# Turning the left halves of three normalized residuals by DMA instead of on TensorE

## The chip, the cores and the metric

The kernel runs on one core of a Trainium2 chip. The metric is device time in microseconds. Five engines work side by side, each through its own queue of instructions in order, and meet by semaphores: TensorE (PE in the profile, with its weight loads as PEld), VectorE (DVE), ScalarE (ACT), GpSimd (POOL) and SyncE (SP), whose queue here issues nearly all DMAs.

## What is computed

One decoder layer on 256 tokens of width 2048, in float32. The residual h passes a half SwiGLU, a mixing block (a gated MLP and sliding-window attention side by side), a cross-attention to 256 memory rows, a second half SwiGLU and a final norm:

```python
def reference(x, mem, ...):
    h = x
    for l in range(DEPTH):                                   # DEPTH = 1
        h = h + 0.5 * swiglu(rmsnorm(h, g_ffn1[l]), w1_gate[l], w1_up[l], w1_down[l])
        z = rmsnorm(h, g_mix[l]) @ w_in[l]
        ...
        h = h + y @ w_out[l]
        h = h + cross_attention(rmsnorm(h, g_x[l]), rmsnorm(mem, g_mem[l]),
                                w_xq[l], w_xkv[l], w_xo[l])
        h = h + 0.5 * swiglu(rmsnorm(h, g_ffn2[l]), w2_gate[l], w2_up[l], w2_down[l])
    return rmsnorm(h, g_final)
```

Three of these norms matter here. The kernel calls their results n2 (g_mix, between the down projection f1d of the first SwiGLU and the projection q), n3 (g_x, between the output projection wo of the mixing block and the query projection xq) and n4 (g_ffn2, between xo, the output projection of the cross-attention, and f2g, the gate and up projection of the second SwiGLU).

## The kernel before

**Matrix products.** A product with a weight is cut into *units* of 1024 output columns, and a unit into *chunks*: one chunk is 256 rows of the weight as four blocks of 128x512, 1 MB, loaded by SP. Full precision is had by splitting each operand into a high and a low part: ACT casts a weight block to wh (L147), DVE subtracts to get wl (L148), and three matmuls are done (high by high, low by high, high by low). Of the weights three chunks can be loaded ahead, and two can be cast ahead. The other operand is a *pair*: two 128-row pieces of the transposed activations, four 128x128 blocks, again as high and low parts (names with fh and fl, for n2 n2fh and n2fl).

**Kinds of chunks.** N is the plain product of two-by-two blocks (24 matmuls). S is a chunk by seven products in the manner of Strassen (21 matmuls); it needs sums of weight blocks (DVE makes t from L337 to L341, ACT casts it to th, DVE makes tl) and sums of activation blocks. C stands between them. In an S chunk, and in the first and last chunk of a unit, the third matmul already reads wl; in the others the wl passes come last. wo has two units of eight chunks, with the kinds NNNNNSNN and NNNSNSNN; xo has the same. The last unit of f1d has the kinds NNSNSNN.

**PSUM.** Eight banks: four for results that are read at a unit's end, four ("tr") for the products that are read early and for transposes. At the end of a unit DVE adds the results to h. The products P1, Q5, Q6 and Q7 of S chunks are read early: ACT copies P1 (wop, L627), DVE forms wov and woz from it and adds them to h (names f1dp, f1dv, f1dz in f1d; xop, xov, xoz in xo).

**The norms.** next_norm builds n2, n3 and n4 as the columns of h become final. A unit of f1d, wo or xo finishes one half of h: the first (columns 0 to 1023, blocks j = 0 and 1) is ready one unit before the other. When the left half is final, its squares give a provisional scale; scaled(j) multiplies 512 columns of h by it on ACT (L834, tile n2s, n3s or n4s), and make(j) turns them: for each of two pairs PE makes four transposes of 128x128 (L248, against ident), and ACT brings them from PSUM with the gain (L266). So while the last unit of f1d, wo or xo runs, four pairs of the left half are made beside it; the four of the right half follow in the next unit.

**Order.** PE's order is that of the code (it alone is pinned). Two lists set where other work goes in it. Side work (side_add) is run in steps between groups of six matmuls. The list later holds pairs of a count and a function; turn, called once a chunk, runs those whose count is 0 and takes 1 from the others. On ACT, DVE, POOL and SP a scheduler sets the order of instructions when the program is built; on the chip each queue keeps it.

**Turning by DMA, as f1 does it already.** The results of gate and up, and the memory keys, are not transposed on PE: turned_rows splits each float32 into two 16-bit halves on ACT (L153, a 128x1024 copy), SP issues a transposing DMA (L156), and two 128x512 copies a pair (L691) put the halves together again.

Of the kernel before, what the change touches and what calls it, by code (L numbers as in the profile page):

```python
# [33 lines left out]
def layer_kernel(  # L34
# [43 lines left out]
    def s2(s):  # L78
        return tmp.tile([P, 512], F32, tag="s2", name=nm(s))
# [84 lines left out]
    def words_of(raw, n):  # L164
        return raw.bitcast(U16).rearrange("p (i t h) -> p i t h", i=n, h=2)
# [74 lines left out]
    def laid(kind, k, tb):  # L240
        return BASE[kind].index(f"A{tb + 1}{k + 1}")
# [9 lines left out]
    def row_tile(kind, v, k):  # L251

        return v[:, k::2, :] if kind == "C" else v[:, 2 * k:2 * k + 2, :]

    def pair_from_rows(s, kind, src, gcol):
        ps = transposed(s, kind, src)
        p = Pair(s, kind)
        if kind != "N":
            raw = s2(s + "r").rearrange("p (k t) -> p k t", k=4)
        for k in range(2):  # L260
            g = sm[:, gcol + k:gcol + k + 1]
            if kind == "N":
                hi, lo = [row_tile("N", t, k) for t in p.base]
                split_scaled(hi, lo, row_tile("N", ps, k), g)
            else:
                nc.scalar.activation(row_tile(kind, raw, k), row_tile(kind, ps, k), AF.Copy, scale=g)  # L266
        if kind != "N":
            fill(s, p, raw)
        return p
# [171 lines left out]
    def side_add(gen):  # L441
        side.append([now[0], gen])
# [357 lines left out]
    def next_norm(s, gcol, kinds="NNNNNNNN"):  # L800

        mixed = "S" in kinds
        parts = tiny.tile([P, TB, NG], F32, tag="parts", name=nm("parts"))
        pairs = [None] * 8
        done = [0] * NG
        st = {}  # L810

        def on_block(j, tb):
            square_into(parts[:, tb, j:j + 1], h[:, tb, j * 512:(j + 1) * 512], 512)
            done[j] += 1
            if not mixed:
                if done[j] == TB:
                    make(j, lambda tb, c: h[:, tb, c:c + P])
            elif j < 2:
                if done[0] + done[1] == 2 * TB:
                    st["est"] = rstd_of(parts[:, :, :2], 2, 1024)  # L820

                    def first():
                        yield 1
                        for i in range(2):
                            scaled(i)

                    side_add(first())
            elif done[j] == TB:
                scaled(j)

        def scaled(j):
            r = m4(s + "s").rearrange("p (b c) -> p b c", b=TB)
            for tb in range(TB):
                nc.scalar.activation(  # L834
                    r[:, tb], h[:, tb, j * 512:(j + 1) * 512], AF.Copy, scale=st["est"][:, tb:tb + 1]
                )
            make(j, lambda tb, c: r[:, tb, c - j * 512:c - j * 512 + P])

        def make(j, src):
            def work():  # L840
                for i in (2 * j, 2 * j + 1):
                    yield 4 if i % 2 == 0 and mixed else 1
                    pairs[i] = pair_from_rows(
                        s, kinds[i], lambda tb, k: src(tb, (2 * i + k) * P), gcol + 2 * i
                    )

            side_add(work())

        def rs():
            if "rs" not in st:  # L850
                st["rs"] = rstd_left(parts, st["est"]) if mixed else rstd_of(parts, NG, D)
            return st["rs"]

        return pairs, on_block, rs
# [655 lines left out]
```

## Time and profile before

| | |
|---|---|
| median of 3 runs | 2034.7 us (2034.1 to 2034.9) |
| the profiled execution | 2033.6 us, span 2031.9 us |
| granted TensorE clock | 0.999 |
| instructions on PE, DVE, ACT | 9203, 1994, 1460 |
| DMA | 415.83 MB, mean 205 GB/s |

The span runs from the first to the last instruction of the profiled execution; its own time is 1.7 us longer. Three stretches of it matter: the end of f1d (about 655 to 715 us from the start), the end of wo (1088 to 1150) and the end of xo (1290 to 1372). Rows of a timeline give start, duration, engine, line, operation, output and inputs; the bracket at the end tells how long the engine was idle before, and what ended that. Instructions on one engine overlap a little, so what one costs in its queue is read from the next one's start.

### The profile page before, as it was taken

The page shows a single profiled execution, that of the slowest core. Times are in us where ns is not written, and L with a number is a line of the kernel's source. Part 1 is how long each engine was busy: PE and PEld are TensorE (multiplying, and loading weights), DVE is VectorE, ACT ScalarE, POOL GpSimd, SP SyncE. Part 2 cuts the span into 40 slices and gives each one's busy share as a digit, 9 for nine tenths or more (in the row PEclk, how much of TensorE's full clock was granted, in tenths as well). Part 3 has the DMA queues.
Part 4 walks back from the last instruction along what each step waited for, and adds up shares of the span by engine and source line. Part 5 has one row for each costly group of instructions (what it writes and reads, how often), then busy time and mean ns, then how long its engine had stood idle before and what let it go on. Part 6 is the DMA issues. An engine that isn't in the chain of part 4 may idle for free.

```text
span 2031.9 us, 24271 instructions
## 1 busy us (share of the span) xinstructions
PE 2015.5 (99%) x9203; PEld 1668.8 (82%) x9203; DVE 1853.6 (91%) x1994; ACT 1313.2 (65%) x1460; POOL 34.4 (2%) x57
## 2 busy tenths in 40 slices
PE   9999999999999999999999999999999999999998
PEld 7788888888888888888888888888888888888886
DVE  6999999999999978989879987899999999999998
ACT  7765566567665766755566666676656666676664
POOL 0000000000000010200000000000000000000000
PEclk9999999999999999999999999999999999999999
DMA  8666666666556575544675544556566656665563
GB/s 312 197 206 225 215 218 205 236 209 220 196 191 219 177 252 178 202 166 166 208 227 182 198 160 145 187 187 224 197 239 215 215 205 231 214 219 206 187 228 125
DMA packets 115333, 415.83 MB, mean 205 GB/s; under 512 B 61824, under 2 KB 63888, under 8 KB 68112
## 3 DMA queue, kind: packets, MB, share of 16 engines
q1 hardware_dynamic: 112768, 407.14, 57.6%
q0 software_dynamic: 2016, 6.30, 1.0%
q8 instruction: 72, 1.18, 0.2%
q10 hardware_dynamic: 432, 0.84, 0.1%
q14 instruction: 45, 0.37, 0.1%
HBM read 398.52 MB, written 2.10 MB: 197 GB/s over the span
## 4 chain that ended last, share of the span: by engine, by line
PE 85%; DVE 9%; issue 3%; ACT 2%; DMA 2%; SPq 0%; POOL 0%; POOLq 0%; DVEq 0%; ACTq 0%
PE f1gQ L428 12%; PE f2gQ L428 12%; PE f2dQ L428 6%; PE f1dQ L428 6%; PE f1gP L428 5%; PE f2gP L428 4%; PE xqQ L428 3%; PE f2dP L428 3%; PE f1dP L428 3%; PE woQ L428 2%; PE xoQ L428 2%; PE f2dR L428 2%; PE f1dR L428 2%; DVE f1gwl L148 2%; PE vQ L428 2%
## 5 line engine op out<-in xcount | busy, mean ns | idle before, releaser
L148 DVE TENSOR_TENSOR f1gwl<-f1gw,f1gwh 128x1536 fp32r<-128x1536 f32 (+2 forms) x94 | 181.6, 1934 | 24.5 <-ACT f1gwh L147 23.8
L147 ACT CAST f2gwh<-f2gw 128x1536 fp32r<-128x1536 f32 (+1 forms) x88 | 150.5, 1712 | 66.4 <-PE f2gQ L428 44.9
L148 DVE TENSOR_TENSOR f2gwl<-f2gw,f2gwh 128x1536 fp32r<-128x1536 f32 (+1 forms) x88 | 179.1, 2036 | 8.0 <-ACT f2gwh L147 8.0
L147 ACT CAST f1gwh<-f1gw 128x1536 fp32r<-128x1536 f32 (+2 forms) x94 | 153.1, 1629 | 45.0 <-PE f1gQ L428 19.3
L147 ACT CAST f1gth<-f1gt 128x1024 fp32r<-128x1024 f32 x76 | 79.9, 1051 | 103.1 <-DVE f1gt L337 68.7
L147 ACT CAST f2gth<-f2gt 128x1024 fp32r<-128x1024 f32 x82 | 85.4, 1050 | 64.2 <-DVE f2gt L341 34.0
L428 PE MATMUL f2gQ<-f2gwh,n4fh 128*128 128x512 f32 x317 | 123.8, 390 | 0.6 <-DVE f2gv L587 0.6
L428 PE MATMUL f2gQ<-f2gwh,n4fl 128*128 128x512 f32 x317 | 123.4, 389 | 0.0
L428 PE MATMUL f1gQ<-f1gwh,n1fl 128*128 128x512 f32 x286 | 111.4, 390 | 1.7 <-DVE n1fl L148 1.7
L428 PE MATMUL f1gQ<-f1gwh,n1fh 128*128 128x512 f32 x286 | 111.6, 390 | 0.0
L147 ACT CAST f2dwh<-f2dw 128x2048 fp32r<-128x2048 f32 (+1 forms) x44 | 77.4, 1758 | 47.5 <-PE f2dQ L428 39.5
L147 ACT CAST f1dwh<-f1dw 128x2048 fp32r<-128x2048 f32 (+1 forms) x44 | 77.3, 1757 | 43.7 <-PE f1dQ L428 42.7
L148 DVE TENSOR_TENSOR f1dwl<-f1dw,f1dwh 128x2048 fp32r<-128x2048 f32 (+1 forms) x44 | 92.0, 2092 | 12.0 <-ACT f1dwh L147 11.8
L148 DVE TENSOR_TENSOR f2dwl<-f2dw,f2dwh 128x2048 fp32r<-128x2048 f32 (+1 forms) x44 | 92.0, 2091 | 11.2 <-ACT f2dwh L147 11.1
L148 DVE TENSOR_TENSOR f2gtl<-f2gt,f2gth 128x1024 fp32r<-128x1024 f32 x82 | 99.5, 1218 | 1.0
L428 PE MATMUL f2gQ<-f2gwl,n4fh 128*128 128x512 f32 x317 | 96.7, 389 | 0.0
L148 DVE TENSOR_TENSOR f1gtl<-f1gt,f1gth 128x1024 fp32r<-128x1024 f32 x76 | 92.2, 1216 | 0.5
L428 PE MATMUL f1gQ<-f1gwl,n1fh 128*128 128x512 f32 x286 | 86.9, 389 | 0.0
L428 PEld LDWEIGHTS f2gQ<-f2gwh,n4fh 128*128 128x128 f32 x317 | 59.5, 188 | 13.8 <-DVE f2gv L587 1.6
L428 PEld LDWEIGHTS f2gQ<-f2gwh,n4fl 128*128 128x128 f32 x317 | 59.5, 188 | 12.2
L428 PEld LDWEIGHTS f2gQ<-f2gwl,n4fh 128*128 128x128 f32 x317 | 59.4, 188 | 12.3
L428 PE MATMUL f2gP<-f2gwh,n4fh 128*128 128x512 f32 x176 | 68.6, 390 | 0.0
(824 smaller groups left out, 6072.2 us busy)
## 6 DMA issues: line engine op xcount, KB each, us to landing
f2gw<-in_w_gu SPq DMA_DIRECT2D x88, 1024.0 KB, 4.9
f1gw<-in_w_gu SPq DMA_DIRECT2D x86, 1024.0 KB, 4.8
f1dw<-in_w_down SPq DMA_DIRECT2D x44, 1024.0 KB, 4.8
f2dw<-in_w_down SPq DMA_DIRECT2D x44, 1024.0 KB, 4.8
wow<-in_w_out SPq DMA_DIRECT2D x16, 1024.0 KB, 4.8
xqw<-in_w_xq SPq DMA_DIRECT2D x16, 1024.0 KB, 4.8
xow<-in_w_xo SPq DMA_DIRECT2D x16, 1024.0 KB, 4.8
qw<-in_w_in SPq DMA_DIRECT2D x8, 1024.0 KB, 4.8
```

The source lines that it names most:

```text
L147: nc.scalar.copy(hi, src)
L148: nc.vector.tensor_tensor(lo, src, hi.bitcast(F32), ALU.subtract)
L428: nc.tensor.matmul(self.banks[name], x, y, start=name not in self.begun, stop=self.left[name] == 0)
```

## The change

The left halves of n2, n3 and n4 take the way by DMA. scaled(j) for j = 0 and 1 calls turned_rows for both token blocks instead of make; a new function pair_joined puts the halves together, scales them by the gain in place, and fills the pair. These steps are no side work any more: scaled(0) and scaled(1) are put in the list later with the counts 0 and 1, and each puts its two pairs there with the counts 1 and 2. The right halves are made as before. Lines behind the new function move by 21 or 27 (L627 becomes L648, L834 becomes L850).

```diff
+    def pair_joined(s, kind, turned, c, gcol):
+        raw = s2(s + "r")
+        words = words_of(raw, 4)
+        for tb in range(TB):
+            j, k = laid(kind, 0, tb), laid(kind, 1, tb)
+            nc.scalar.copy(words[:, j:k + 1:k - j], by_block(turned)[:, tb, c:c + 2])
+        raw = raw.rearrange("p (k t) -> p k t", k=4)
+        p = Pair(s, kind)
+        for k in range(2):
+            g = sm[:, gcol + k:gcol + k + 1]
+            src = row_tile(kind, raw, k)
+            if kind == "N":
...
+            else:
+                nc.scalar.activation(src, src, AF.Copy, scale=g)
+        if kind != "N":
+            fill(s, p, raw)
+        return p
...
                     st["est"] = rstd_of(parts[:, :, :2], 2, 1024)
-                    def first():
-                        yield 1
-                        for i in range(2):
-                            scaled(i)
-                    side_add(first())
+                    for i in range(2):
+                        later.append((i, lambda i=i: scaled(i)))
...
-            make(j, lambda tb, c: r[:, tb, c - j * 512:c - j * 512 + P])
+            if j > 1:
+                make(j, lambda tb, c: r[:, tb, c - j * 512:c - j * 512 + P])
+                return
+            t = tile_turned(s + "t")
+            for tb in range(TB):
+                turned_rows(s, t[:, tb], r[:, tb])
+            def pair(i):
+                pairs[i] = pair_joined(s, kinds[i], t, 2 * (i % 2), gcol + 2 * i)
+            for i in (2 * j, 2 * j + 1):
+                later.append((1 + i % 2, lambda i=i: pair(i)))
```

**What moves on the engines.** On PE 48 transposes go, 16 in each of the three places, and the rest keeps its order. On ACT and DVE the scheduler's order changes around them. First ACT in the last unit of f1d, when the left half of h is final: n2s is the scaled left half, f1dwh_5286 (before) and f1dwh_5315 (after) the cast of the weights of chunk 2, an S chunk. Before:

```order
L147 CAST f1dwh_5246<-f1dw_5245 128x2048
L834 ACTIVATE n2s_5267<-h,rs_5243 128x512 x2
L834 ACTIVATE n2s_5270<-h,rs_5243 128x512 x2
L147 CAST f1dwh_5286<-f1dw_5285 128x1536
L147 CAST f1dth_5299<-f1dt_5289 128x1024
L147 CAST f1dwh_5362<-f1dw_5361 128x2048
```

The same place after the change; n2w are the 16-bit halves, n2t what the transposing DMA writes, n2r the halves joined:

```order
L147 CAST f1dwh_5256<-f1dw_5255 128x2048
L850 ACTIVATE n2s_5245<-h,rs_5243 128x512 x2
L153 COPY n2w_5249<-n2s_5245 128x1024
L153 COPY n2w_5252<-n2s_5245 128x1024
L850 ACTIVATE n2s_5289<-h,rs_5243 128x512 x2
L153 COPY n2w_5293<-n2s_5289 128x1024
L153 COPY n2w_5296<-n2s_5289 128x1024
L277 COPY n2r_5299<-n2t_5248 128x512
L147 CAST f1dwh_5315<-f1dw_5314 128x1536
L147 CAST f1dth_5328<-f1dt_5318 128x1024
```

Four copies and one that waits for a transposing DMA now stand between n2s and the S chunk's cast.

Second, DVE at the end of wo, before: wov and woz come from the early products, the last four adds to h (from woP, woQ, woR and woQ) are the results of the unit's last chunk, and xqwl is the low part of the first weights of the next unit, xq.

```order
L628 SCALAR_TENSOR_TENSOR wov_9118<-woQ_1806_9026,wop_1818_9117 128x512
L621 SCALAR_TENSOR_TENSOR h<-woQ_1804_9024,h 128x512
L631 SCALAR_TENSOR_TENSOR woz_9119<-woQ_1805_9025,wov_9118 128x512
L621 SCALAR_TENSOR_TENSOR h<-woQ_1804_9024,h 128x512
L639 TENSOR_TENSOR h<-h,wov_9118 128x512
L640 TENSOR_TENSOR h<-h,woz_9119 128x512
L641 TENSOR_TENSOR h<-h,woz_9119 128x512
L148 TENSOR_TENSOR xqwl_9161<-xqw_9159,xqwh_9160 128x2048
L621 SCALAR_TENSOR_TENSOR h<-woP_1757_8839,h 128x512
L621 SCALAR_TENSOR_TENSOR h<-woQ_1758_8840,h 128x512
L621 SCALAR_TENSOR_TENSOR h<-woR_8841,h 128x512
L621 SCALAR_TENSOR_TENSOR h<-woQ_1760_8842,h 128x512
```

DVE at the same place after the change, from woz on:

```order
L652 SCALAR_TENSOR_TENSOR woz_9123<-woQ_1809_9029,wov_9122 128x512
L232 TENSOR_TENSOR n3f_9013<-n3r_9004,n3f_9013 128x128
L659 TENSOR_TENSOR h<-h,wop_1822_9121 128x512
L660 TENSOR_TENSOR h<-h,wov_9122 128x512
L642 SCALAR_TENSOR_TENSOR h<-woP_1763_8851,h 128x512
L642 SCALAR_TENSOR_TENSOR h<-woQ_1764_8852,h 128x512
L148 TENSOR_TENSOR n3fl_9010<-n3f_9013,n3fh_9009 128x512
L661 TENSOR_TENSOR h<-h,woz_9123 128x512
L662 TENSOR_TENSOR h<-h,woz_9123 128x512
L642 SCALAR_TENSOR_TENSOR h<-woR_8853,h 128x512
L642 SCALAR_TENSOR_TENSOR h<-woQ_1766_8854,h 128x512
L148 TENSOR_TENSOR xqwl_9165<-xqw_9163,xqwh_9164 128x2048
```

xqwl has moved from ahead of the last four adds to behind them, and pieces of the last left pair (n3f, n3fl) stand among them. At the end of xo the order changes in the same way, with f2gwl in xqwl's place; at the end of f1d qwl keeps its place ahead of the adds.

Third, ACT at the end of wo before, where wowh are the casts of chunks 6 and 7 and xqwh is the first cast of xq:

```order
L147 CAST wowh_9091<-wow_9090 128x2048
L627 ACTIVATE wop_1818_9117<-woP_1803_9023 128x512
L147 CAST wowh_9130<-wow_9129 128x2048
L147 CAST xqwh_9160<-xqw_9159 128x2048
L137 ACTIVATE junk_9190,parts_8415<-h 128x512
```

The same place after:

```order
L147 CAST wowh_9095<-wow_9094 128x2048
L147 CAST n3fh_8950<-n3r_8947 128x512
L147 CAST n3fh_8952<-n3f_8956 128x256
L277 COPY n3r_9004<-n3t_8882 128x2x256 x2
L147 CAST wowh_9134<-wow_9133 128x2048
L287 ACTIVATE n3r_9004<-n3r_9004,sm 128x256 x2
L147 CAST xqwh_9164<-xqw_9163 128x2048
L147 CAST n3fh_9007<-n3r_9004 128x512
L648 ACTIVATE wop_1822_9121<-woP_1807_9027 128x512
```

The evacuation wop, which DVE's wov waits for, has moved from behind chunk 6's cast to behind xqwh. On SP the four transposing DMAs of each norm go among the weight loads: one, a load, then three in a row.

More of the change, by code (lines that the diff above doesn't have):

```diff
@@ L266, in pair_from_rows @@
                 nc.scalar.activation(row_tile(kind, raw, k), row_tile(kind, ps, k), AF.Copy, scale=g)
+        if kind != "N":
[13 more added lines that the diff above has]
+            if kind == "N":
+                hi, lo = [row_tile("N", t, k) for t in p.base]
+                split_scaled(hi, lo, src, g)
+            else:
+                nc.scalar.activation(src, src, AF.Copy, scale=g)
         if kind != "N":
```

## The prediction

> **What bounds the kernel now.** The page first: busy time by engine.
>
> ```profile
> span 2031.9 us, 24271 instructions
> PE 2015.5 (99%) x9203; PEld 1668.8 (82%) x9203; DVE 1853.6 (91%) x1994; ACT 1313.2 (65%) x1460; POOL 34.4 (2%) x57
> ```
>
> PE is idle for 16 us of the span, so a microsecond less of matmul is a microsecond less of time, as long as nothing makes PE wait. DVE at 91% and ACT at 65% feed it: each chunk of weights is cast by ACT (wh), and DVE makes the remainder (wl). Next, PE's timeline where left halves are transposed now, at the end of f1d's last unit (start, duration, instruction):
>
> ```profile
> 672.52 0.62 PE L428 MATMUL f1dP<-f1dwl,f1afh 128*128 128x512 f32 x2
> 672.98 0.60 PE L248 MATMUL n<-ident,n2s 128*128 128x128 f32 x4
> 673.34 0.70 PE L428 MATMUL f1dQ<-f1dwl,f1afh 128*128 128x512 f32 x2
> 673.88 0.63 PE L428 MATMUL f1dR<-f1dwl,f1afh 128*128 128x512 f32 x2
> ...
> 675.16 0.48 PE L428 MATMUL f1dP<-f1dwh,f1afh 128*128 128x512 f32 x1
> 675.48 0.40 PE L428 MATMUL f1dP<-f1dwh,f1afl 128*128 128x512 f32 x1
> 675.71 0.40 PE L428 MATMUL f1dP<-f1dwl,f1afh 128*128 128x512 f32 x1
> ```
>
> Starts tell more than durations: a pair of 512-wide matmuls costs 672.98 - 672.52 = 0.46 us, one 0.23. A group of four transposes holds the queue for 673.34 - 672.98 = 0.36, and the pair behind it takes 673.88 - 673.34 = 0.54, 0.09 too long: **0.45 us a group**. At 675.16 an S chunk begins, and its third matmul, 0.55 later, already reads wl. So a late wl stops PE at once.
>
> **What the change takes away.** Twelve groups (four pairs in each of n2, n3, n4): 12 x 0.45 = 5.4 us of PE. The view of the transposes' tile adds who waits for them:
>
> ```profile
> L248 PE MATMUL n<-ident,n4s x32: 270/272/276, 1302.8 to 1351.4; 128*128 128x128 f32 x32
>   PEld xoQ L428: 1.6, 1
> ```
>
> Of these 32 half go. The one wait is in xo's S chunk, which needs a PSUM bank that n4's evacuation holds; the next rows show it, and a wait in q for its second chunk's cast.
>
> ```profile
> 1314.16 0.39 PE L428 MATMUL xoQ<-xoth,xofl 128*128 128x512 f32 x1
> 1315.72 0.50 PE L428 MATMUL xoQ<-xoth,xofh 128*128 128x512 f32 x1 [1.17 <-ACT n4r L266]
> ...
> 707.30 0.39 PE L428 MATMUL qQ<-qwl,n2fh 128*128 128x512 f32 x1
> 707.88 0.50 PE L428 MATMUL qP<-qwh,n2fh 128*128 128x512 f32 x1 [0.19 <-ACT qwh L147]
> ```
>
> 1.56 - 0.23 = 1.3 us goes with the bank; 0.58 - 0.23 = 0.35 goes if PE reaches that chunk later, as it will below. **Taken away: 7.1 us.**
>
> A rule stands against the change: the Trainium skill, VectorE: DVE Perf Modes, section Rules for kernel authors, says to transpose 128x128 on TensorE where PSUM will do. With the 390 ns of its section The three transpose paths, 48 would be worth an estimated 18.7 us, and the sum below would come out 4 us faster. The rows above give 0.11 us each; the trace decides, and the sum keeps 5.4.
>
> **What it adds.** Per norm, ACT gets four copies of 128x1024 halves and eight of 128x512; the scalings only change their source. SP gets four transposing DMAs. Prices from their like in f1 and mk:
>
> ```profile
> 226.78 1.04 ACT L153 COPY f1w<-f1gp 128x1024 uint16<-128x1024 uint16 x1
> 227.72 1.04 ACT L153 COPY f1w<-f1gz 128x1024 uint16<-128x1024 uint16 x1
> 482.07 1.85 ACT L691 COPY f1r<-f1a 128x512 uint16<-128x512 uint16 x3
> f1a<-f1w SPq DMA_TRANSPOSE x22, 3.2
> L156 SPq DMA_TRANSPOSE mkT<-mkw x8: 1237/1316/4127, 1005.5 to 1054.2; - x8
> DMA to landing us min/median/max: 3.2/5.3/6.6
> ```
>
> A large copy takes 0.94 us of ACT's queue (start to start), a small one 0.6: 4 x 0.94 + 8 x 0.6 = 8.6 us a norm. ACT has such idle time on average, but not where the copies stand. I follow the queue at each place.
>
> *n2, the S chunk.* Rows of ACT, then DVE:
>
> ```profile
> 667.65 2.57 ACT L834 ACTIVATE n2s<-h,rs 128x512 f32<-128x512 f32 x4 [0.55 <-POOL rs L132]
> 670.12 1.46 ACT L147 CAST f1dwh<-f1dw 128x1536 fp32r<-128x1536 f32 x1
> 671.62 1.76 DVE L148 TENSOR_TENSOR f1dwl<-f1dw,f1dwh 128x1536 fp32r<-128x1536 f32 x1 [2.19 <-ACT f1dwh L147]
> ```
>
> Now the cast begins at 670.12; in the changed order four copies and one L277 copy stand ahead of it: 667.65 + 2.47 + 4 x 0.94 + 0.6 = 674.5. It ends at 676.0, wl at 676.0 + 1.76 = 677.75. PE, rid of two groups, wants wl at 675.71 - 0.90 = 674.8. **Stall 2.95 us.** Behind the cast wait the T casts and chunk 3's wh (679.3, wanted at 682): no more stalls there. The L277 copy needs the first transposing DMA, issued about 670.1, landed at 673.3 by the 3.2 above and 676.7 by the longest 6.6; I take the short one, as only one load overlaps, and keep 2.8 us for the range. SP's loads pass: each issue is 1.3 us of its queue (4.1 at most), the next loads are wanted 10 us later.
>
> *n2, the unit's end.* What a piece costs on ACT and where q begins on PE:
>
> ```profile
> 674.54 0.82 ACT L266 ACTIVATE n2r<-n,sm 128x256 f32<-128x256 f32 x2
> 675.40 0.62 ACT L147 CAST n2fh<-n2r 128x512 fp32r<-128x512 f32 x1
> 679.01 1.05 ACT L147 CAST f1dth<-f1dt 128x1024 fp32r<-128x1024 f32 x1
> 702.09 0.39 PE L428 MATMUL qP<-qwh,n2fh 128*128 128x512 f32 x1
> ```
>
> f1dp (the evacuation of product P1) had its place right behind chunk 5's cast; now all pair work and q's first cast stand ahead of it. From 679.3 on that is four pairs of n2r (0.8 each), three more weight casts (1.4, 1.8, 1.8), two f1dth (0.95), seven n2fh (0.5 or 0.3), six L277 copies (0.6): 16.7 us, to 696.0; then q's cast 1.8 and f1dp 0.6: 698.5. DVE, which has qwl to do first (to 700.4), needs f1dv, f1dz, a remainder and two adds before it reads f1dP's bank, free at 704.05. PE wants that bank for q at 702.09 - 1.8 + 2.95 = 703.2, so it waits 0.85, and 0.25 more for the last bank. **1.1 us**, the upper end; the lower is 0, with the bank free in time.
>
> *n3, wo to xq.* Same steps: the S chunk first.
>
> ```profile
> 1098.11 2.56 ACT L834 ACTIVATE n3s<-h,rs 128x512 f32<-128x512 f32 x4
> 1109.51 0.39 PE L428 MATMUL woP<-wowl,yafh 128*128 128x512 f32 x1
> ```
>
> 1098.11 + 6.85 = 1104.95, cast to 1106.4, wl to 1108.3; wanted at 1109.51 - 1.8 = 1107.7. Stall 0.6. Then the end of wo, DVE's and PE's rows:
>
> ```profile
> 1129.86 2.28 DVE L148 TENSOR_TENSOR xqwl<-xqw,xqwh 128x2048 fp32r<-128x2048 f32 x1
> 1132.06 0.68 DVE L621 SCALAR_TENSOR_TENSOR h<-woP,h 128x512 f32<-128x512 f32 x1
> 1132.66 0.68 DVE L621 SCALAR_TENSOR_TENSOR h<-woQ,h 128x512 f32<-128x512 f32 x1
> ...
> 1135.10 0.69 DVE L621 SCALAR_TENSOR_TENSOR h<-woQ,h 128x512 f32<-128x512 f32 x1 [0.67 <-PE woQ L428]
> 1134.90 0.39 PE L428 MATMUL xqP<-xqwh,n3fh 128*128 128x512 f32 x1
> 1135.35 0.39 PE L428 MATMUL xqP<-xqwl,n3fh 128*128 128x512 f32 x1
> 1127.85 1.92 ACT L147 CAST xqwh<-xqw 128x2048 fp32r<-128x2048 f32 x1 [4.61 <-PE woQ L428]
> ```
>
> Before, xqwl is done ahead of the last four adds to h. In the changed order **it stands behind them**, and the last add can't start before wo's last matmul. So even a punctual DVE makes PE wait: add at 1135.10, xqwl at 1135.7 to 1138.0, against 1135.35: 2.7 us, the lower end. DVE isn't punctual: wop stands behind xqwh on ACT, which PE releases at 1127.85 - 1.1 = 1126.7 and which ends at 1128.5; a cast of n3fh and wop follow, to 1129.6. Then on DVE, 0.6 each for wov, woz and two adds, 0.2 for two small n3f (1132.5), seven more of 0.6 (1136.75), xqwl 2.28: 1139.0. PE has ended wo at 1133.8 and wants wl at 1134.25. Stall 4.8, the value I take, as every row of its walk is from this place. **n3: 5.5** with 0.1 for the chunk before.
>
> *n4, xo to f2g.* The same orders, 202.4 us later, and f2gwl behind the adds too. ACT and DVE have more to do here:
>
> ```profile
> 1300.50 2.56 ACT L834 ACTIVATE n4s<-h,rs 128x512 f32<-128x512 f32 x4
> ...
> 1308.84 0.40 ACT L147 CAST n4more<-n4d 128x256 fp32r<-128x256 f32 x1
> 1327.07 1.28 ACT L93 ACT_TABLE_LOAD   x1
> ```
>
> The first S chunk loses 0.6 as in wo. The second loses 2.1: ACT has its cast at 1318.6, but on DVE pieces of n4 stand ahead of xowl, whose sources ACT delivers until 1320.0, so that xowl ends at 1322.95 and is wanted at 1320.85. (In wo the same sum gives 1118.25 against 1118.5: just in time.) The last chunk, whose third matmul also reads wl, loses 0.8. What PE has lost by then, DVE has won: at f2g's third matmul 3.1 are left of wo's 4.8. **n4: 6.6**, between 2.7 (the forced wait alone) and 6.6.
>
> **Sum.** Stalls 2.95 + 1.1 + 5.5 + 6.6 = 16.1, taken away 7.1: 9 us slower. The profiled execution took 2033.6 us (span 2031.9, 1.7 around it), 1.1 below the median of 2034.7; 2033.6 + 9 = 2042.6, on the median **2043.7**.
>
> **Rivals.**
> 1. *PE waits only for what the order forces*: 2.2 at n2 (the cast a little earlier), 2.7 at each handover, the rest hidden. 7.6 - 7.1 = +0.5: 2035.2, and up to 2038.8 if half the lateness shows. For: DVE idles 2.19 us ahead of f1dwl, so it has some slack. Against: the queues are in order and ACT's rows leave no gap to catch up in.
> 2. *Faster*: the saved PE time arrives whole because ACT's and DVE's lateness stays under cover. 2034.7 - 7.1 = 2027.6. It decides at f1dwl ready by 674.8 and xqwl ready by 1134.25; that needs wl ahead of the adds. For it: PE is 99% busy. Against it: the order of DVE's rows. [...]
> 3. *Transposing DMAs land late*, 6.6 us instead of 3.2, and ACT waits in its queue: 2.8 us more at n2, 2.6 at n3 and n4: 2043.7 + 8 = 2051.7.
>
> **How the numbers follow.** Forecast 0.70, rival 3 or part of it 0.11, rival 1 0.13, rival 2 0.06. The range from 2035.2 to 2051 leaves out the faster case and the end of rival 3. Measurement can tell about 0.2%, 4.1 us, from no change: faster 0.06, same 0.14 (rival 1), slower 0.80.
>
> **What would show it.** Right: 48 transposes fewer in the tile's view; PE idle about 3 us at 674 to 678 with DVE f1dwl as its releaser, and 3 to 5 us at the third matmul of xq and of f2g, released by xqwl and f2gwl; xoQ's wait for n4r gone. Wrong: those third matmuls start 0.45 us after the first, or ACT waits for n2t, n3t or n4t before its L277 copies.

## The result, and the profile after

The changed kernel takes **2055.5 us** (median of 4 runs, 2055.07 to 2055.76) against 2034.4 us before, beside it on the same chip: a ratio of 1.0104 (95% interval 1.0091 to 1.0116), 21 us slower. The forecast was 2043.7, with a range to 2051.0. The direction was right and the size was not.

The page of the changed kernel, its span and its engines:

```profile
span 2053.8 us, 24225 instructions
PE 2020.3 (98%) x9155; PEld 1665.9 (81%) x9155; DVE 1854.7 (90%) x1994; ACT 1338.0 (65%) x1496; POOL 35.6 (2%) x57
```

48 transposes are gone (9203 to 9155), and PE is busy 5 us *longer*. So some matmuls took longer, beside PE idling more. The view of what PE waited for (total us, times, longest) shows where it idles; first the changed kernel, the largest rows but for those of the first chunks:

```profile
PE xqP L449 <- DVE xqwl L148: 4.5, 1, 4.5
PE xoP L449 <- DVE xowl L148: 3.4, 2, 2.5
PE f2gP L449 <- DVE f2gwl L148: 2.5, 1, 2.5
...
PE f2gQ L449 <- DVE f2gv L608: 1.6, 4, 0.9
PE f1dP L449 <- ACT f1dwh L147: 1.5, 1, 1.5
PE f2gQ L449 <- ACT f2gth L147: 1.4, 1, 1.4
...
PE woP L449 <- DVE wowl L148: 1.2, 2, 0.7
...
PE f1dP L449 <- DVE f1dwl L148: 1.1, 1, 1.1
PE qP L449 <- DVE qwl L148: 0.9, 1, 0.9
```

and the same view before, where these places have only:

```profile
PE xoQ L428 <- ACT n4r L266: 1.2, 1, 1.2
...
PE f2gQ L428 <- DVE f2gv L587: 0.6, 2, 0.3
...
PE f2gP L428 <- DVE f2gwl L148: 0.3, 1, 0.3
...
PE qP L428 <- ACT qwh L147: 0.2, 1, 0.2
```

The bank wait for n4r went, as forecast. New waits are where the forecast had put them, and in places where it had none: once in q (qwl), between wo's and between xo's S chunks (wowh and xowh, 0.5 each), at f2gth, and further on in f2g (f2gv, 1.6 in place of 0.6).

PE's timeline at the S chunk of n2, and at the handover to xq:

```profile
675.38 0.50 PE L449 MATMUL f1dP<-f1dwh,f1afh 128*128 128x512 f32 x1 [1.50 <-ACT f1dwh L147]
675.71 0.40 PE L449 MATMUL f1dP<-f1dwh,f1afl 128*128 128x512 f32 x1
677.17 0.79 PE L449 MATMUL f1dP<-f1dwl,f1afh 128*128 128x512 f32 x1 [1.06 <-DVE f1dwl L148]
677.76 0.63 PE L449 MATMUL f1dP<-f1dwh,f1afh 128*128 128x512 f32 x1
678.19 0.63 PE L449 MATMUL f1dP<-f1dwh,f1afl 128*128 128x512 f32 x1
...
1139.25 0.39 PE L449 MATMUL xqP<-xqwh,n3fl 128*128 128x512 f32 x1
1144.16 0.74 PE L449 MATMUL xqP<-xqwl,n3fh 128*128 128x512 f32 x1 [4.52 <-DVE xqwl L148]
1144.70 0.63 PE L449 MATMUL xqP<-xqwh,n3fh 128*128 128x512 f32 x1
1145.13 0.63 PE L449 MATMUL xqP<-xqwh,n3fl 128*128 128x512 f32 x1
```

Two things are to be seen. One is the waits: 1144.16 - 1139.25 - 0.23 = 4.68 us at xq. The other is that behind them matmuls start 0.43 us apart (678.19 - 677.76, 1145.13 - 1144.70) where they start 0.227 apart elsewhere. The table by stretch says why; its columns are the stretch, its length, busy time of PE, PEld, DVE, ACT and POOL, then the granted clock, and DMA:

```profile
677.00:680.00 3.00, 2.83 (x7) 2.25 (x8) 2.48 (x3) 2.07 (x2) 0.00 (x0) 0.50 1.18 219
...
1144.00:1147.30 3.30, 3.14 (x8) 2.46 (x9) 2.87 (x6) 1.20 (x2) 0.17 (x1) 0.54 0.60 204
...
1339.00:1342.00 3.00, 3.00 (x8) 2.32 (x8) 2.84 (x3) 3.00 (x5) 0.00 (x0) 0.50 0.40 164
...
1357.40:1361.00 3.60, 3.60 (x16) 2.95 (x17) 2.66 (x5) 1.27 (x4) 0.61 (x1) 1.00 0.73 253
```

The granted clock is half behind the waits in n2, at xq and in xo, and full behind the 2.5 us wait at f2g. In all, 25 matmuls ran at 0.427: 25 x 0.2 = **5.0 us** that no wait shows.

The account from start to start of all of PE's instructions, each against the usual pitch of its shape, counting excesses over 0.06 us: 48.5 us of waits against 27.7 before, so +20.8; +5.0 for the slow clock; -5.4 for the twelve groups of transposes. That is 20.4 of the 21.9 us between the two spans; the rest lies in smaller steps.

### The profile page after: what moved, and what is told of

Same layout as the page of the kernel before. It is cut to its first block, busy times and chain, and to the rows that moved or that the text cites. A ratio compares the mean times of both kernels' runs of the same rounds, so it can differ in the third digit from the quotient of the medians.

```text
span 2053.8 us, 24225 instructions
## 1 busy us (share of the span) xinstructions
PE 2020.3 (98%) x9155; PEld 1665.9 (81%) x9155; DVE 1854.7 (90%) x1994; ACT 1338.0 (65%) x1496; POOL 35.6 (2%) x57
## 4 chain that ended last, share of the span: by engine, by line
PE 70%; issue 16%; DVE 9%; ACT 3%; DMA 3%; POOL 0%; SPq 0%; POOLq 0%; DVEq 0%; ACTq 0%
PE f2gQ L449 13%; PE f1gQ L449 11%; PE f2dQ L449 6%; PE f2gP L449 5%; PE f1gP L449 4%; PE xqQ L449 3%; PE f2dP L449 3%; PE f2dR L449 2%; PE xoQ L449 2%; DVE f1gwl L148 2%; PE vQ L449 2%; PE mv0Q L449 2%; PE mv1Q L449 2%; PE mk1Q L449 1%; PE mk0Q L449 1%
## 5 line engine op out<-in xcount | busy, mean ns | idle before, releaser
L148 DVE TENSOR_TENSOR f1dwl<-f1dw,f1dwh 128x2048 fp32r<-128x2048 f32 (+1 forms) x44 | 92.1, 2093 | 16.4 <-ACT f1dwh L147 16.1
```

Source lines behind the costliest of these rows:

```text
L148: nc.vector.tensor_tensor(lo, src, hi.bitcast(F32), ALU.subtract)
```

## The experiments

Each ratio is to the kernel before, beside it on the same chip (2033.9 to 2034.8 us). Diffs are against the changed kernel unless said otherwise; "..." stands for lines left out.

### The handover to xq and f2g

The first chunk's load and split are put ahead in the scheduler's order:

```diff
-        b = load(u.s, w, u.kinds[i], pieces, ...)
+        if i == 0 and u.s in ("xq", "f2g"):
+            with tc.high_priority():
+                b = load(u.s, w, u.kinds[i], pieces, ...)
+        else:
+            b = load(u.s, w, u.kinds[i], pieces, ...)
```

> The changed kernel, with the load and split of the first chunk of xq and of f2g put ahead in the order, so that DVE has xqwl and f2gwl before the last four adds to h; the copies stay on ACT. Theory (the wait at the handover is forced by that order): the 4.7 us at xq's third matmul, the 2.7 us at f2g's and the slow clock behind xq's, 1.6 us, go: 2046.5 us, up to 2049 if the adds, 2.2 us later, hold a PSUM bank. The waits in n2's and n4's S chunks stay as they are. Rival (ACT's queue is so late that the wait shows up in any order): 2053 us or more, with xqwh in place of the adds ahead of xqwl.

Measured: 2048.2 us, ratio 1.0068 (1.0055 to 1.0080), 7 us under the changed kernel. xqwl is no longer waited for; the adds it overtook hold PE's bank instead, for less, and the clock stays up:

```profile
1141.65 0.47 PE L449 MATMUL xqP<-xqwh,n3fh 128*128 128x512 f32 x1 [1.36 <-DVE h L646]
1141.95 0.40 PE L449 MATMUL xqP<-xqwh,n3fl 128*128 128x512 f32 x1
1142.19 0.39 PE L449 MATMUL xqP<-xqwl,n3fh 128*128 128x512 f32 x1
```

The prediction's reading of this place holds: that wait was made by DVE's order.

The same for all weights of f1d, wo and xo, and for q's first chunk (the diff is against the run above):

```diff
-        if i == 0 and u.s in ("xq", "f2g"):
+        if u.s in ("f1d", "wo", "xo") or i == 0 and u.s in ("q", "xq", "f2g"):
```

> The changed kernel, with loads and splits of the weights of f1d, wo and xo, and of the first chunk of q, xq and f2g, put ahead of all side work in the order; copies stay on ACT. Theory (it is the copies' place ahead of the casts that costs, not their sum): the waits for f1dwh, wowl, xowl, xqwl and f2gwl go, what is left is pairs that come late at the start of q, xq and f2g: 2038 us, between 2030 and 2046. Rival (ACT has no room for them anywhere in these stretches): as much wait at other places, 2050 us or more.

Measured: 2053.7 us, 1.0096 (1.0083 to 1.0110). The rival: the S chunks no longer wait, but PE waits 9.6 us at the start of f2g for the last adds to h. More priority moved the lateness here and didn't remove it.

### What a long wait does to the clock

```diff
+            if self.s in ("xq",) and not self.begun:
+                name, x, y = steps[0]
+                for _ in range(14):
+                    nc.tensor.matmul(self.banks[name], x, y, start=True, stop=True)
             self.run(steps + behind)
```

> The changed kernel, with the first matmul of xq (xqP from xqwh and n3fh) done 14 times more ahead of the chunk, each overwriting the bank: 14 x 0.227 = 3.2 us more work for PE, all of it inside the 4.7 us wait for xqwl. Theory (a long wait costs its length and then a slower clock, since behind it seven 512-wide matmuls have a pitch of 0.427 in place of 0.227 us): with the wait down to 1.5 us the pitch behind it stays 0.227, and the time falls by 7 x 0.2 + 0.2 = 1.6 us to 2053.9, though work was added. Rival (the slow pitch has another cause, a port or late data): pitch 0.427 stays and the time is the same, 2055.5, or higher.

At the place itself it came out to the tenth: from xq's first matmul to the first of its second chunk took 11.87 us in the changed kernel and 10.25 with 14 matmuls *more*, 1.62 less. PE's rows behind the added ones:

```profile
1143.34 0.39 PE L453 MATMUL xqP<-xqwh,n3fl 128*128 128x512 f32 x1
1145.08 0.50 PE L453 MATMUL xqP<-xqwl,n3fh 128*128 128x512 f32 x1 [1.35 <-DVE xqwl L148]
1145.41 0.40 PE L453 MATMUL xqP<-xqwh,n3fh 128*128 128x512 f32 x1
1145.65 0.39 PE L453 MATMUL xqP<-xqwh,n3fl 128*128 128x512 f32 x1
```

Behind the shorter wait the pitch is 0.24. The kernel as a whole took longer: 2057.9 us (2054.1 to 2058.7), 1.0110 (1.0094 to 1.0125). One reason is in the edit. Its condition holds at the start of each of xq's two units, so 28 matmuls were added (PE has 9183, the changed kernel 9155), and the second 14, from 1188.81 to 1191.99 us, stand where PE waits for nothing: 3.2 us that the forecast of 2053.9 doesn't count. With them it would have been 2057.1.

The clock fits xq's other traces too. Three kernels wait 4.5 us there and have 6 to 8 slow matmuls behind; five wait 1.3 to 1.9 us and have none. But this trace has a full clock in n2 as well, behind the same waits of 1.5 and 1.1 us as in the changed kernel, and a halved one at f2g, behind the same 2.5 us, and the edit touches neither. So that a shorter wait keeps the clock up is shown at xq; what the slow clock costs the whole kernel is known from the traces alone, and differs between executions.

### One norm at a time

The diff for n3; n2 and n4 likewise:

```diff
-                    for i in range(2):
-                        later.append((i, lambda i=i: scaled(i)))
+                    if s in ("n3",):
+                        for i in range(2):
+                            later.append((i, lambda i=i: scaled(i)))
+                        return
+
+                    def first():
+                        yield 1
+                        for i in range(2):
+                            scaled(i)
+
+                    side_add(first())
...
-            if j > 1:
+            if j > 1 or s not in ("n3",):
```

> Only n3's left halves are turned by transposing DMAs; n2 and n4 as in the kernel before. From the trace of the changed kernel: 7.3 us of added waits around n3 (0.5, 0.6, 0.9 and 4.7 among them), 1.6 us of slow clock, 1.8 us of transposes less: 7 us slower, 2041.5 us. Rival (lateness is handed on from norm to norm, so that one norm alone costs little): 2036 to 2038 us, with xq's wait down to 2.7 us.

> Only n2's left halves are turned by transposing DMAs; n3 and n4 as in the kernel before. From the trace of the changed kernel: 4.9 us of added waits (1.7 and 1.2 in the S chunk, 1.2 in q), 1.6 us of slow clock, 1.8 us of transposes and 0.35 of an old wait less: 4.3 us slower, 2038.5 us. Rival (what is slower in n2 stays hidden later on): within 2 us of before, 2036 or less.

> Only n4's left halves are turned by transposing DMAs; n2 and n3 as in the kernel before. From the trace of the changed kernel: 6.9 us of waits up to the handover to f2g, 4.1 in f2g behind it, 2.8 us of slow clock, 1.8 us of transposes and 1.3 of the old bank wait less: 10.7 us slower, 2045 us; with the runs of n2 and of n3 alone the three then add up to the whole. Rival (n4 inherits lateness from n2 and n3): 2041 us or less, and the three sum to clearly less than the whole, 21.1 us.

Measured: n3 alone 2042.4 us, 1.0038 (1.0025 to 1.0050); n2 alone 2042.1, 1.0037 (1.0024 to 1.0049); n4 alone 2045.9, 1.0060 (1.0046 to 1.0074). All three cost by themselves. But 8.3 + 8.0 + 11.8 = 28 us is more than the 21 of the whole, not less, as the rival had it. n2 alone is the odd one: its trace is only 3 us behind when it enters f2g, and another 3 are lost inside f2g at 1545 to 1553, long after n2. Why f2g loses more there than in the kernel with all three stays open.

### Which of ACT's work: the copies

The twelve copies a norm on GpSimd:

```diff
-    def turned_rows(s, dst, src):
+    def turned_rows(s, dst, src, copy=nc.scalar.copy):
...
-        nc.scalar.copy(
+        copy(
...
-            nc.scalar.copy(words[:, j:k + 1:k - j], by_block(turned)[:, tb, c:c + 2])
+            nc.gpsimd.tensor_copy(words[:, j:k + 1:k - j], by_block(turned)[:, tb, c:c + 2])
...
-                turned_rows(s, t[:, tb], r[:, tb])
+                turned_rows(s, t[:, tb], r[:, tb], nc.gpsimd.tensor_copy)
```

> The changed kernel, with the twelve added 16-bit copies of each norm (four of 128x1024, eight of 128x512) issued on GpSimd in place of ACT; nothing else is edited, the transposing DMAs and the places of the steps stay. Theory (ACT's queue is what makes the weights late): with 8.6 us of copies a norm gone from ACT, the casts of the S chunks stand where they stood before, xqwl and f2gwl stand ahead of the last four adds on DVE again, no wait of PE over 1 us is left in n2, n3 and n4, and the 7.1 us taken away from PE arrive: 2029 us, between 2027 and 2032, faster than before. Rival (the transposing DMAs land late, or the steps are placed too early or too late): the waits stay, 2045 to 2055. Second rival (GpSimd copies take several times ACT's 0.94 and 0.6 us): the pairs come late, PE waits for n2fh, n3fh or n4fh, over 2034 us.

Measured: 2057.7 us, 1.0113 (1.0100 to 1.0127). A miss for the theory. The second rival explains it; the groups by line, mean ns of one behind the busy us:

```profile
L153 POOL COPY n3w<-n3s 128x1024 uint16<-128x1024 uint16 x4 | 9.0, 2289 | 1.2 <-ACT n3s L850 1.2
L277 POOL COPY n2r<-n2t 128x512 uint16<-128x512 uint16 x8 | 8.8, 1143 | 0.6 <-DMA n2t<-n2w 0.6
```

against ACT's 1035 and 678 ns. ACT now waits in its queue for n2r (4.5 us at 674 to 679), with casts behind it. Since the move made the copies slower too, it doesn't tell whether ACT's copies were the cause. The next run leaves the copies out, and with them the turning; the DMAs still run, but the pairs are made from the rows:

```diff
-                turned_rows(s, t[:, tb], r[:, tb])
+                nc.sync.dma_start_transpose(t[:, tb], r[:, tb].bitcast(U16))
...
-            for tb in range(TB):
-                j, k = laid(kind, 0, tb), laid(kind, 1, tb)
-                nc.scalar.copy(words[:, j:k + 1:k - j], by_block(turned)[:, tb, c:c + 2])
...
-                nc.scalar.activation(src, src, AF.Copy, scale=g)
+                nc.scalar.activation(src, turned[:, :, (c + k) * P:(c + k + 1) * P], AF.Copy, scale=g)
...
-                pairs[i] = pair_joined(s, kinds[i], t, 2 * (i % 2), gcol + 2 * i)
+                pairs[i] = pair_joined(s, kinds[i], r, 2 * (i % 2), gcol + 2 * i)
```

> The changed kernel without its twelve 16-bit copies a norm on ACT: the transposing DMAs are issued at their places and read the scaled rows as they are, and the pairs are scaled from those rows without being transposed; so the turning itself is left out, everything else stays. Theory (the 8.6 us of copies a norm on ACT are what makes the weights late): the waits of PE go, the 7.1 us taken away arrive: 2028 us, between 2027 and 2031. Rival (the places of the steps by chunk count, or SP's issues of the transposing DMAs ahead of the weight loads): waits stay, 2040 us or more.

Measured: 2040.3 us, 1.0036 (1.0024 to 1.0049). Without the copies 15 us are gone, and that part of the theory holds. The edit takes one more thing away: the pairs no longer wait for the DMAs to land, for which ACT waits 1.7, 1.7 and 2.1 us in the changed kernel. How much of the 15 us is that wait isn't shown. And the 7.1 us didn't arrive: the kernel is 6 us slower than before *without* the copies. What remains was first put down to the places of the steps.

### The places, and what is left without anything added

The old places, taken between matmuls:

```diff
-                    for i in range(2):
-                        later.append((i, lambda i=i: scaled(i)))
+                    def first():
+                        yield 1
+                        for i in range(2):
+                            scaled(i)
+
+                    side_add(first())
...
-            for i in (2 * j, 2 * j + 1):
-                later.append((1 + i % 2, lambda i=i: pair(i)))
+            def work():
+                for i in (2 * j, 2 * j + 1):
+                    yield 4 if i % 2 == 0 else 1
+                    pair(i)
+
+            side_add(work())
```

> The turning by DMA alone: copies on ACT and transposing DMAs as in the changed kernel, but the steps are taken between matmuls where the kernel before took them (held back in the S chunks), not by the count of chunks. Theory (two causes: the copies, some 15 us by the run without them, and pairs bunched into S chunks by the count, some 13 us by what that run kept): the second goes, 2042 us, between 2038 and 2047. Rival (only the copies on ACT count, wherever they stand): 2053 to 2057 us as the changed kernel.

> As the last, and without the twelve 16-bit copies a norm on ACT: the pairs are scaled from the rows without being transposed, so the turning itself is left out; the transposing DMAs are still issued. Theory (copies and places are the whole cost): the waits in n2, n3 and n4 go and 7.1 us are gained: 2028 us, 2026.5 to 2030. Rival (the transposing DMAs cost by themselves, on SP's queue or by their traffic): the run without copies kept its 2040 for that reason, and this one stays above 2034.

> The turning by DMA at the old places, and the first chunk of xq and of f2g split ahead of the last four adds. Theory: the two gains add, as the handover wait is forced by the order of DVE alone: 6 us under the run with the old places only, about 2036 us (2032 to 2041). Rival (the handover wait is made by ACT's lateness, which the old places have already taken away): the same time as the run with the old places alone.

The pairs spread further, by `later.append((2 + i - j, ...))`, with the first chunk ahead:

> The changed kernel with its four pairs of a norm spread over four chunks (counts 2, 3, 4, 5 behind the estimate, in place of 1, 2, 2, 3), and the first chunk of xq and of f2g split ahead of the adds. Theory (pairs bunched into S chunks make the weights late): 2043 us, below the 2048.2 of the run with the first chunk ahead alone, by 4 us or more. Rival (the sum of ACT's work counts, not its bunching): 2047 to 2050 us.

Measured: 2056.7 us, 1.0110 (1.0096 to 1.0124); without copies 2041.3, 1.0033 (1.0021 to 1.0046); with the first chunk ahead 2048.2, 1.0068 (1.0055 to 1.0081); spread 2051.0, 1.0081 (1.0067 to 1.0095), no better than the 2048.2 without spreading. Four misses for "bunched steps": as long as copies or DMAs are there, the old places give the time of the new within 1 us or so.

Then all that was added is left out, and only PE's transposes stay away. Against the two kernels without copies, the transposing DMAs go as well:

```diff
-            t = tile_turned(s + "t")
-            for tb in range(TB):
-                nc.sync.dma_start_transpose(t[:, tb], r[:, tb].bitcast(U16))
```

> The kernel before with the 48 transposes of PE left out and nothing in their place: no copies, no transposing DMAs, steps at the old places; the pairs are scaled from the rows without being transposed, so the turning is left out. It differs from the run with old places and no copies by the twelve DMAs alone. Theory (the transposing DMAs stand on SP's queue ahead of the load of the next S chunk's weights, whose issue came at 1310.5 in place of 1303.0 us in that run, so the weights are late): the 7.1 us arrive, 2028 us. Rival (the pair steps, no longer held back by transposes on PE, run ahead of the casts): as that run, 2038 to 2042 us.

> The same without copies, DMAs and transposes, but the steps placed by the count of chunks as in the changed kernel. If the places by count cost something by themselves: 2032 us or more. If not, the same 2028 us as at the old places. Rival of both (pair steps not held back by PE): 2038 to 2042 us.

Measured: bare at the old places 2036.1 us, 1.0009 (1.0000 to 1.0017), between the two forecasts; by the count 2039.0, 1.0026 (1.0015 to 1.0036). This is the finding of the study. **48 transposes less, nothing in their place, and the kernel is not faster.** The two profiled executions lie further apart, 5.1 us, and 3.0 of it is slow clock: 15 slow matmuls by the count, none at the old places. What PE waits for in the bare kernel at the old places:

```profile
PE xoQ L445 <- DVE xotl L148: 2.3, 1, 2.3
...
PE woP L445 <- DVE wowl L148: 1.5, 1, 1.5
...
PE qP L445 <- DVE qwl L148: 1.4, 1, 1.4
```

Each norm's gain is taken back a few chunks on, by a remainder that DVE hands over late. With two smaller ones, for xowl and f2gtl, these waits are 7.5 us from start to start. Beside the runs without copies these two also price the transposing DMAs: 4.3 us at the old places (6.5 over before, to 2.2) and 1.1 by the count (6.2 to 5.1). The two prices aren't shown to differ: the slow clock is in one trace of each couple only (15 slow matmuls with DMAs at the old places, 15 in the bare kernel by the count), and the waits alone differ by about 3 and 2 us. The DMAs hold SP while weights are due. SP's rows in xo, of the kernel before and then with DMAs at the old places and no copies:

```profile
1302.95 0.33 SPq L335 DMA_DIRECT2D xow<-in_w_xo  x1
1306.63 8.72 SPq L358 DMA_DIRECT2D xow<-in_w_xo  x2
```

```profile
1302.16 8.21 SPq L859 DMA_TRANSPOSE n4t<-n4s  x4
1310.47 0.52 SPq L352 DMA_DIRECT2D xow<-in_w_xo  x1
```

The load goes out 7.5 us later, and DVE waits for it:

```profile
1316.10 1.23 DVE L354 TENSOR_TENSOR xot<-xow 128x1024 f32<-128x1024 f32 x1 [2.74 <-DMA xow<-in_w_xo]
```

### The two additions alone, on the kernel before

Against the kernel before, with PE's transposes kept:

```diff
+            if j < 2:
+                halves16 = r.bitcast(U16).rearrange("p b (c t) -> p b c t", c=8)
+                for tb in range(TB):
+                    w = s2(s + "w").bitcast(U16)
+                    nc.scalar.copy(...)
...
+                    if halves16 is not None:
+                        d = words_of(s2(s + "d"), 4)
+                        for tb in range(TB):
+                            a, b = laid(kinds[i], 0, tb), laid(kinds[i], 1, tb)
+                            c = 2 * (i % 2)
+                            nc.scalar.copy(d[:, a:b + 1:b - a], by_block(halves16)[:, tb, c:c + 2])
```

> The kernel before, PE's transposes kept, with the twelve 16-bit copies a norm on ACT added ahead of them (their results are not used). Theory (8.6 us of copies a norm in ACT's queue cost what the run without copies gained, 15 us): 2049 us, 2044 to 2053. Rival (copies cost only together with the DMAs that wait for them): 2037 us or less.

```diff
+                t = tile_turned(s + "t")
+                for tb in range(TB):
+                    nc.sync.dma_start_transpose(t[:, tb], r[:, tb].bitcast(U16))
```

> The kernel before, PE's transposes kept, with the four transposing DMAs a norm issued by SP as soon as the rows are scaled (their results are not used). Theory (issue on SP's queue ahead of the weight loads): 8 to 13 us slower, 2042 to 2047 us, with ACT or DVE waiting for f1dw, wow or xow to land. Rival (SP's queue has room): 2034 to 2036 us.

Measured: copies 2057.2 us, 1.0112 (1.0096 to 1.0127), above the range given; DMAs 2039.7, 1.0026 (1.0017 to 1.0035), between the two forecasts. In the trace of the DMAs most of it is one wait in xo, 3.5 us in place of 1.2 for the same bank, with 12 slow matmuls behind it. In the trace of the copies, where PE's transposes are kept, the copies delay the evacuation of a bank as well, and PE waits at each:

```profile
1120.49 0.50 PE L428 MATMUL woQ<-woth,yafh 128*128 128x512 f32 x1 [2.93 <-ACT n3r L266]
...
1124.99 0.79 PE L428 MATMUL woQ<-woth,yafh 128*128 128x512 f32 x1 [3.77 <-ACT n3r L266]
```

### What takes the 7 us back

In the S chunks DVE's three sums are left out, in the bare kernel at the old places and, as the control, in the kernel before:

```diff
-            t = stream.tile([P, 4, 512], F32, tag="t", name=nm(s + "t"), bufs=1)
-            nc.vector.tensor_tensor(...)
-            nc.vector.tensor_tensor(t[:, 2, :], t[:, 0, :], raw[:, 2, :], ALU.add)
-            nc.vector.tensor_tensor(t[:, 3, :], t[:, 2, :], raw[:, 3, :], ALU.add)
+            if s in ("f1d", "wo", "xo", "q", "xq"):
+                t = raw
+            else:
+                ...
```

> The bare kernel at the old places (no transposes, copies or DMAs), and in the S chunks of f1d, wo, xo, q and xq the three sums T on DVE are left out (the raw weights stand in their place), which takes 2.6 us of DVE from each such chunk. Theory (the 7.1 us do not arrive in the bare kernel because DVE hands over wl and the T remainders no earlier than before): with DVE ahead they do arrive, 2028 us, 2026.5 to 2030. Rival (ACT's casts or the order of the steps hold PE back, not DVE): 2034 to 2036 as the bare kernel.

> The kernel before with the same sums left out. Theory (here PE sets the time in these stretches, so less work for DVE is worth nothing): 2033.5 us, 2032.5 to 2034.5. Rival (DVE sets the time here too): 2028 to 2031 us.

Measured: bare **2028.3 us**, 0.9973 (0.9963 to 0.9982); before 2033.5, 0.9998 (0.9989 to 1.0007). The same relief of DVE is worth nothing while PE has its transposes, and 8 us without them. So it is by way of DVE that the 7 us are lost. The stretch 1305 to 1335 by engine, columns as above; the kernel before, bare, bare with less for DVE, and the control:

```profile
1305.00:1335.00 30.00, 28.83 (x132) 23.53 (x131) 29.86 (x39) 21.66 (x28) 0.00 (x0) 1.00 0.59 215
```

```profile
1305.00:1335.00 30.00, 27.08 (x119) 21.77 (x118) 29.38 (x35) 20.68 (x26) 0.00 (x0) 1.00 0.55 201
```

```profile
1305.00:1335.00 30.00, 30.00 (x134) 24.86 (x133) 26.19 (x35) 21.78 (x32) 0.21 (x1) 1.00 0.54 199
```

```profile
1305.00:1335.00 30.00, 30.00 (x137) 24.60 (x136) 26.74 (x37) 19.34 (x26) 0.00 (x0) 1.00 0.57 200
```

Before the change DVE is busy 29.86 of 30 us here. With transposes off PE, PE is busy less and DVE about as much as before. In the third PE is busy all the time. In the control it is too, and its time is that of the kernel before: one stretch of PE doesn't tell the time of the whole.

A full DVE isn't the only thing that makes a remainder late. The scheduler also ordered DVE anew. At the end of wo, the kernel before and then the bare one, the last wowl and wov, which is made from early products:

```profile
1123.45 2.28 DVE L148 TENSOR_TENSOR wowl<-wow,wowh 128x2048 fp32r<-128x2048 f32 x1
1125.66 0.68 DVE L628 SCALAR_TENSOR_TENSOR wov<-woQ,wop 128x512 f32<-128x512 f32 x1
```

```profile
1121.56 0.68 DVE L645 SCALAR_TENSOR_TENSOR wov<-woQ,wop 128x512 f32<-128x512 f32 x1
...
1126.36 2.28 DVE L148 TENSOR_TENSOR wowl<-wow,wowh 128x2048 fp32r<-128x2048 f32 x1
```

In the bare kernel wowl stands behind wov and seven more instructions for the early products, and PE wants it at 1127.0. Its cast was done at 1120.3, so with these behind it, it would have been ready at 1121.56 + 2.28 = 1123.8. In q, qwl has likewise gone behind three adds, and in xo two adds stand ahead of the last xotl. An estimate from these rows: up to 1.6 + 1.7 + 1.2 = 4.5 of the 7.5 us of waits are order, and the rest isn't explained by it. With less work for DVE, wowl and qwl stand ahead of the adds again, so that run doesn't tell order and load apart; none here keeps the order fixed.

None of the versions that do all of the work is faster than the kernel before.

## Why the prediction was wrong, step by step

The runs split the 21 us, each kernel taken against the runs of the kernel before beside it. In the order of the count: transposes away and steps by the count, +5.1 us (2039.0); transposing DMAs, +1.1 (2040.3, from 6.2 over before); copies and the wait for landing, +14.9 (to 21.1 over). At the old places: +2.2, +4.3, +15.5.

- **"Taken away: 7.1 us" is the step that failed**, and with it the sentence it rests on, that a microsecond less of matmul is a microsecond less of time as long as nothing makes PE wait. The work did leave PE: 5.4 us of transposes and the two old waits are gone from its rows. It wasn't time: the bare kernels are +2.2 us at the old places and +5.1 by the count, so 9 to 12 us of the forecast's miss of 12. The proviso was written down and not checked for the kernel *without additions*: DVE hands the remainders over too late there, by its load, by its new order, or by both. 91% of DVE is a mean over the span; at 1305 to 1335 it was 29.86 of 30, and in the other two stretches, before the change, 95%:

```profile
680.00:700.00 20.00, 20.00 (x93) 16.56 (x93) 19.02 (x22) 10.88 (x14) 0.00 (x0) 1.00 0.54 203
1110.00:1136.00 26.00, 26.00 (x116) 21.55 (x115) 24.72 (x29) 15.30 (x22) 0.00 (x0) 1.00 0.55 199
```

- **The same miss on PE's own account**: the changed kernel's new waits are 22.5 us (20.8 and the 1.7 that went) where 16.1 were forecast, and the slow clock is 5.0 where nothing was. What the bare runs add is that 9 to 12 us of lateness come with no copy and no DMA, partly at other places.
- **The stalls, 16.1 us together, have the size of what the runs give copies and DMAs** (14.9 and 1.1, or 15.5 and 4.3). That is partly luck, for the waits in the trace hold the bare kernel's lateness too, and errors cancel. At their places, by starts less 0.227, the large ones fit: n2's S chunk 1.66 + 1.23 = 2.89 against 2.95 forecast (one wait for wh, one for wl); xq's third matmul 4.68 against 4.8; f2g's 2.69 against 3.1; xo's second S chunk 2.72 against 2.1, its first 1.04 against 0.6. ACT's walk in n2, the cast at 674.5, came at 673.86, behind the copies as forecast:

```profile
673.28 0.68 ACT L277 COPY n2r<-n2t 128x512 uint16<-128x512 uint16 x1
673.86 1.47 ACT L147 CAST f1dwh<-f1dw 128x1536 fp32r<-128x1536 f32 x1
```

- **Misses among them**: the bank at q's start (1.1 forecast) cost nothing, and xo's last chunk (0.8) neither; wo lost 0.6 ahead of its second S chunk and 0.9 in it, xo 0.9 ahead of its own, q 1.1 at 740, f2gth 1.6 at 1385, and f2gv 1.4 more than before further on.
- **The clock was left out**: a wait was priced at its length. Behind three places slow matmuls cost up to 2.6 us more (13 x 0.2), 5.0 in all in this execution.
- **"SP's loads pass" was wrong in kind**: with the DMAs and no copies, at the old places, four transposing DMAs held SP 8.2 us in xo and the weights came late. In the changed kernel they hold it as long (n4: 1.23 and then 7.40 us), but what that costs there isn't shown; by the count the DMAs are 1.1 us, within the noise.
- **Rival 2, faster at 2027.6**, is out even without copies or DMAs: the bare kernel gives 2036.1. With DVE relieved as well it gives 2028.3, near that number. The Trainium skill, Perfetto Trace Analysis, section Identifying the Most-Contended Engine, would have the engine with the highest occupancy optimized first, but judges TensorE by MFU and by the busy share of its weight loads, and not by that of its matmuls. The weight loads' share is 82% here against DVE's 91%; by that measure DVE would come first and not PE, and the runs agree: the 48 transposes off PE are worth something only with DVE relieved.
- **Rival 3, late landing**: this was also one of the prediction's own signs of being wrong, and in part it came. ACT waited for n2t, n3t and n4t 1.7, 1.7 and 2.1 us, 5.5 in all against the rival's 8. The rival's 2051.7 is the nearest of the numbers given, but how much of the 5.5 us reached PE isn't shown. **Rival 1, only forced waits**, is out by its numbers, 2035.2 to 2038.8; by its own terms the upper end would be 2035.2 + (16.1 - 7.6) / 2 = 2039.4.
- **The rule that spoke against the change** (the Trainium skill, VectorE: DVE Perf Modes, section Rules for kernel authors: transpose 128x128 on TensorE where PSUM will do) came out right, and not for the price of a transpose: most of what the DMA path costs here is its copies, with the wait for landing.

## What to carry to other kernels

Before work is taken off the busiest engine, read the busy time of the others *in the stretch where it is taken off*: DVE at 91% over the span was at 95 to 100% there. A bare run, with the work left out and nothing in its place, gives the ceiling and should come first: here it was no gain at all, before any cost was counted. Then compare the order of the other engines' queues with the one before, for the scheduler may put the work that is waited for behind work that isn't. And price small copies in an in-order queue by what stands behind them: some 26 us of copies cost about 15 us, though ACT is busy only 65% of the span.

## What the chip showed that was not expected

Behind some waits the granted clock halved and 512-wide matmuls ran at 0.427 in place of 0.227 us, in the changed kernel for 5, 7 and 13 matmuls. Waits of 4.5 us (xq), of 1.5 and 1.1 two matmuls apart (n2) and of 2.5 (xo) did it, another of 2.5 (f2g) did not. Over the traces of all these runs, each of the 11 waits of 3.3 us or more has slow matmuls behind it; of those from 2.2 to 3.0 us about half have. The same wait can go either way: 2.44 and 2.29 us in wo and xo halved the clock in the bare kernel by the count and left it full in the run without copies. The Trainium skill, TensorE: Matmul & The Clock Gate, section Part 1: The HAM clock gate, has the clock halved after an idle window of about 3.4 us that runs freely; the 11 long waits agree, while shorter ones that did it, and like ones that didn't, show that the length of a single wait doesn't decide it here. In xq, where matmuls whose results were thrown away cut the wait to 1.35 us, the clock stayed up.

A transposing DMA of 256 KB held SP for 1.23 to 4.56 us in n4, where a 1 MB load of weights takes 0.33 to 0.53.
